# Pinning the low halves of a plain product's weights on VectorE while tiles are converted beside it

## The chip, the cores and the metric

The kernel runs on one core of one Trainium2 chip. The core has a matrix engine (TensorE, PE in the profile), three engines for elementwise work (VectorE or DVE, ScalarE or ACT, GpSimd or POOL) and a queue engine that issues most transfers (SyncE or SP). The metric is the device time of one execution in microseconds.

## The reference

A two-layer encoder over 512 tokens of width 1024, all in float32. Each layer is a mixing block (two kinds of attention in layer 0, a neighbourhood attention in layer 1) followed by the MLP in which the change lies:

```python
def sq_relu_mlp(h, w_up, w_down):
    u = jax.nn.relu(h @ w_up)
    return (u * u) @ w_down

h = h + sq_relu_mlp(rmsnorm(h, norm_ffn[layer]), ffn_w_up[layer], ffn_w_down[layer])
```

`w_up` is 1024 x 4096 and `w_down` 4096 x 1024, so U = (relu(h w_up))² has 32 tiles of 128 columns. The activations are held transposed: a tile is 128 features by 512 tokens.

## The kernel before

**Split operands.** Every float32 operand of a matmul is kept as a high part (rounded to the matmul's format, a copy on ScalarE) and a low part (what the rounding left, a subtraction). A product is three matmuls: high weights by high x, high weights by low x, low weights by high x (`mm3`, L501 to L503). The low part of a weight chunk thus has to be ready one third of the way into the first step that uses it.

**Two kinds of product.** A *plain* product (`product`) takes its weights in chunks of two k tiles by 512 columns: `chunk` loads 128 x 1024 values into `raw` (L190, SyncE, four buffers), copies the high half to `whi` on ScalarE (L212) and subtracts the low half into `wlo` on VectorE (L202); `whi` and `wlo` have three buffers each, shared by all products. A chunk is eight column-and-k steps of three matmuls. A *seven* product (`Seven`) uses a Strassen-like scheme with seven half-size products on pairs of tiles instead of eight (matmuls L388 to L390); its weight chunks are prepared by `seven_chunk` (GpSimd sums L302 to L304, ScalarE L308, VectorE L309), and its result is put together from four banks by `Seven.run` (ScalarE L396, then four VectorE additions L397 to L400).

**The MLP.** `mlp(l)` makes U in three groups and multiplies each group by its rows of `w_down` as it comes. In the third group (z == 2) things overlap. Its `stage` makes the U tiles by seven products. In layer 0 these are 8 tiles for a plain product and then 10 as raw pairs, R; in layer 1, 6 for the plain product, then 8 as raw pairs, R, and at the end 4 more tiles. A raw pair (`raw_evac`) gets a relu and a square on ScalarE (L1148, L1149); a pair that becomes U tiles (`pair_evac`) also gets a high copy on ScalarE (L833) and a low subtraction on VectorE (L830) for each tile. So the last pair before the plain product is a raw one in layer 0 and one with splits in layer 1.

Then the plain product runs in two generators of four column tiles each (8 chunks in all in layer 0, 6 in layer 1; chunks, and their lows, are numbered from 0 here), and beside it `convert` turns the pairs R into operands of the seven product that follows: for each pair three sums on VectorE (L336, L338, L340) and four splits (high on ScalarE L362, low on VectorE L363). One step of `convert` is written after each of the product's column-and-k steps, seven steps to a pair. `ev` adds the product's finished banks to hT (L1265).

**When a low is written.** Planning a product only lists its chunks. When a step asks for chunk i, `weights` starts the loads up to chunk i + 5 and makes chunks up to i + 2 ready: it writes the high copy and the low subtraction of each. At the first step of the plain product that is chunks 0, 1 and 2; after that one chunk at the first step of each chunk.

**The order on an engine.** The written order is not the order that runs. The framework that builds the kernel orders each engine's instructions by its own model of when their operands will be ready, earlier-written ones first, so an instruction that is ready soon can run before ones written earlier. `tc.keep_in_program_order(op)` takes part of that freedom away: it ties `op` behind the instruction written last before it on the same engine (the order only, with no wait for a result). The sums and the low halves of the splits of `convert` are tied in this way (`held`). The lows of the plain product's chunks (L202) are not. An engine runs its instructions in the order that results.

Of the kernel before, what the change touches and what calls it, by code (L numbers as in the profile page):

```python
# [12 lines left out]
ALU = mybir.AluOpType  # L13
# [17 lines left out]
def f32(ap):  # L31
    return ap.bitcast(F32)
# [3 lines left out]
def encoder_kernel(ctx: ExitStack, tc: tile.TileContext, ins, out, dbg=None):  # L36
    nc = tc.nc
    PE, ACT, DVE, POOL, SP = nc.tensor, nc.scalar, nc.vector, nc.gpsimd, nc.sync
# [22 lines left out]
    def nm(s):  # L61
        cnt[0] += 1
        return f"{s}_{cnt[0]}"
# [119 lines left out]
    def chunk(parts, nk, ncol, heads=None, eng=None, first=False):  # L183

        raw = wp.tile([P, 1024], F32, tag="raw", bufs=4, name=nm("raw"))
        r3 = raw[:, 0 : nk * ncol].rearrange("p (k n) -> p k n", k=nk)
        for lo, n, src in parts:
            dst = r3[:, :, lo : lo + n]
            if len(src.shape) == 3:
                SP.dma_start(dst, src)  # L190
            else:
                for k in range(nk):
                    SP.dma_start(dst[:, k].rearrange("p (z m) -> p z m", z=src.shape[2]), src[:, k])
        yield
        hi = wp.tile([P, 1024], F32R, tag="whi", name=nm("whi"))
        lo_ = wp.tile([P, 1024], F32R, tag="wlo", name=nm("wlo"))
        m = nk * ncol
        v = lambda t: t[:, 0:m].rearrange("p (k n) -> p k n", k=nk)
        lows = []

        def low(to, src, high):
            z = lambda: (eng or DVE).tensor_tensor(to, src, f32(high), op=ALU.subtract)  # L202
            if eng:
                z()
            else:
                lows.append(z)

        if heads is None:
            if first:
                DVE.tensor_copy(hi[:, 0:m], raw[:, 0:m])  # L210
            else:
                ACT.activation(hi[:, 0:m], raw[:, 0:m], AF.Copy)  # L212
            low(lo_[:, 0:m], raw[:, 0:m], hi[:, 0:m])
        else:

            na, nb = heads
            hn = ncol // (na + nb)
            r4 = r3.rearrange("p k (h e) -> p k h e", h=hn)
            for e0, n, o in ((0, na, 0), (na, nb, hn * na)):
                z = [v(t)[:, :, o : o + hn * n].rearrange("p k (h e) -> p k h e", h=hn) for t in (hi, lo_)]  # L220
                src = r4[:, :, :, e0 : e0 + n]
                ACT.activation(z[0], src, AF.Copy)
                low(z[1], src, z[0])
        yield v(hi), v(lo_), lows
# [3 lines left out]


    asked, loaded, ready, low_parts = [], [], [], []  # L230
    AHEAD, LOAD = 2, 5

    def plan(*spec, make=None):
# [230 lines left out]
    def tiles(c0, n):  # L464
        return [(c0 + o, min(P, n - o)) for o in range(0, n, P)]
# [749 lines left out]
    def bias_rows():  # L1215
        R, Fi, Fe = Slot(F32), Slot(F32), Slot(F32)
        rpb = ins["od_rpb"][0]
        for qr in range(8):
            SP.dma_start(R.t[16 * qr : 16 * qr + 16, 0:248],
                           rpb.rearrange("h a b -> h (a b)")[:, (7 - qr) * 31 : (7 - qr) * 31 + 248])  # L1220
            yield
        POOL.memset(Fi.t[:, 0:376], NEG)
        POOL.memset(Fe.t[:, 256:512], NEG)
        rv = R.t[:, 0:248].rearrange("p (k d) -> p d k", d=31)
        POOL.tensor_copy(Fi.t[:, 0:376].rearrange("p (j k) -> p j k", k=8)[:, 15:31, :], rv[:, 7:23, :])
        POOL.tensor_copy(Fe.t[:, 0:248].rearrange("p (j k) -> p j k", k=8), rv)
        for _ in range(6):
            yield
        bxv = bx.rearrange("h t (c r) k -> t c r h k", r=8)
        for c in range(16):  # L1230
            SP.dma_start(bxv[0, c].rearrange("r h k -> r h k"), Fi.t[:, (15 - c) * 8 : (15 - c) * 8 + 256])
            yield

            v, off = (1, (7 - c) * 8) if c < 8 else (0, (23 - c) * 8)
            SP.dma_start(bxv[1, c][:, :, 128 * v : 128 * v + 128], Fe.t[:, off : off + 128])
            yield
            SP.dma_start(bxv[1, c][:, :, 128 - 128 * v : 256 - 128 * v], Fe.t[:, 256:384])
            yield
        for s_ in (R, Fi, Fe):
            s_.free()  # L1240
        yield

    def convert(u7, R):
        held = tc.keep_in_program_order
        for kp, raw in enumerate(R):
            yield from u7.sums(kp, raw, DVE, held)
            yield
            yield from u7.split(kp, held)

    def mlp(l, last=None):  # L1250

        stage, ahead, later = first_product(l)
        w = ins["ffn_w_down"][l]
        bias = bias_rows() if l == 0 else iter(())
        beside = lambda m, i: None
        k0 = 0
        for z, n in enumerate(SIZES[l][:3]):  # L1260
            U, R, V = stage(n, *(SIZES[l][3:] if z == 2 else ()))
            up = [s_.pair() for s_ in U]

            def ev(m, b):
                DVE.tensor_tensor(hT[:, m, :], hT[:, m, :], b, op=ALU.add)  # L1265

            gens = [product(w, k0, up, tiles(512 * c, 512), lambda j, b, c=c: ev(4 * c + j, b)) for c in range(2)]
            k0 += n
            work = iter(())
            if z == 2:  # L1270
                u7 = Seven(2 * len(R))
                ids = [u7.plan(w, 256 * m, k0) for m in range(4)]
                if last:
                    beside = last(k0 + 2 * len(R), V)
                reserve[0] = 8
                work = convert(u7, R)
            else:
                ahead()
            for c, gen in enumerate(gens):
                for i, _ in enumerate(gen):  # L1280
                    if z == 0:
                        later(c, i)
                    elif z == 1:
                        next(bias, None)
                    next(work, None)
            for _ in work:
                pass
            reserve[0] = 1
            for s_ in U:
                s_.free()  # L1290
        for m in range(4):

            def evac(w_):
                h2 = hT[:, 2 * m : 2 * m + 2, :]
                DVE.tensor_tensor(h2, h2, w_.t.rearrange("p (z n) -> p z n", z=2), op=ALU.add)

            for i, _ in enumerate(u7.run(ids[m], evac)):
                beside(m, i)
        u7.free()

    mlp(0)


# [273 lines left out]
    def last_mlp():  # L1577
# [77 lines left out]
        def last(k0, tiles_):  # L1655
# [12 lines left out]
            return beside  # L1668

        mlp(1, last)  # L1670
        for run in runs:
            run()
# [56 lines left out]
```

## Time and profile before

| | |
|---|---|
| median of 3 runs | 1183.68 us (1183.31 to 1185.42) |
| span of the profiled execution | 1184.0 us |
| TensorE busy | 1160.5 us |
| VectorE busy | 883.2 us |
| ScalarE busy | 640.3 us |
| GpSimd busy | 526.1 us |

The page gives no time for the profiled execution beside its span, which lies 0.3 us above the median of the runs. In the layer 0 MLP the plain product of the third group begins 510.46 us into the span, in the layer 1 MLP at 1071.96 us.

How to read the lines that follow. A line of a timeline has the start and the length of an instruction in microseconds, the engine, the line of the kernel, the operation, the tile written and those read by the program's names, the shape, and how many were merged into the line; in brackets stands the idle time just before it and what ended it. A line of the table by windows has the window, its length, then for PE, PEld (weight loads), DVE, ACT and POOL the busy time and the number of instructions, the share of TensorE's clock that was granted, the busy share of the DMA engines and their GB/s. A line of waits has the waiting engine and line, who ended the wait, and total, count and longest. Matmuls are pipelined: the length of one is longer than the distance to the next.

### The profile page before, as it was taken

What the parts mean: (1) busy time and instruction counts of PE and PEld (TensorE: products, weight loads), DVE (VectorE), ACT (ScalarE), POOL (GpSimd) and SP (SyncE); (2) the same over time, 40 slices, a digit from 0 to 9 for tenths busy, and PEclk for the clock granted to TensorE, in tenths of its full rate; (3) what the DMA queues carried; (4) which work ended last, traced back from release to release, by engine and by line L of the source; (5) the groups of instructions that cost most, each with busy time, mean ns of one, the idle gap of its engine ahead of it and who ended that gap; (6) DMA issues with size and microseconds to landing.
All of it is one profiled execution on the core that took longest, in us unless ns stands there. A gap on an engine that the chain in (4) does not pass through costs nothing.

```text
span 1184.0 us, 19784 instructions
## 1 busy us (share of the span) xinstructions
PE 1160.5 (98%) x7128; PEld 1021.2 (86%) x7128; DVE 883.2 (75%) x1514; ACT 640.3 (54%) x1081; POOL 526.1 (44%) x662
## 2 busy tenths in 40 slices
PE   9989999999999999999999999999999999999997
PEld 8667778888899899988998998988889989998895
DVE  5788998878967368786884676667996736778975
ACT  4468676664546247562553565555554624666344
POOL 3267343224562377819602232231376625774710
PEclk9999999999999999999999999999999999999998
DMA  7223225212524723225226464433352341322412
GB/s 244 71 54 92 68 78 134 62 56 77 167 86 134 263 70 90 72 90 165 67 72 178 131 184 126 116 112 109 107 165 76 115 134 55 98 64 89 143 36 71
DMA packets 110145, 128.01 MB, mean 108 GB/s; under 512 B 9075, under 2 KB 86816, under 8 KB 110048
## 3 DMA queue, kind: packets, MB, share of 16 engines
q1 hardware_dynamic: 106992, 119.30, 33.5%
q0 software_dynamic: 2304, 6.31, 2.2%
q8 instruction: 56, 0.92, 0.3%
q10 hardware_dynamic: 752, 1.15, 0.3%
q14 instruction: 41, 0.34, 0.1%
HBM read 104.32 MB, written 6.29 MB: 93 GB/s over the span
## 4 chain that ended last, share of the span: by engine, by line
PE 81%; DVE 4%; ACT 1%; issue 1%; POOL 0%; DVEq 0%; ACTq 0%
PE mm L503 8%; PE mm L501 8%; PE mm L502 8%; PE mm L390 4%; PE mm L389 4%; PE mm L388 4%; PE t L388 3%; PE t L389 3%; PE t L390 3%; PE s L502 2%; PE s L503 2%; PE s L501 2%; PE s L390 2%; PE s L388 2%; PE s L389 2%; PE s L997 2%
## 5 line engine op out<-in xcount | busy, mean ns | idle before, releaser
L309 DVE TENSOR_TENSOR wlo<-a,whi 128x896 fp32r<-128x896 f32 x132 | 161.8, 1230 | 83.7 <-ACT whi L308 82.9
L308 ACT ACTIVATE whi<-a 128x896 fp32r<-128x896 f32 x132 | 125.0, 950 | 155.0 <-PE o L502 45.8
L501 PE MATMUL mm<-a,whi 128*128 128x512 f32 x485 | 195.9, 406 | 0.9 <-DVE a L915 0.7
L503 PE MATMUL mm<-a,wlo 128*128 128x512 f32 x485 | 192.1, 397 | 2.5 <-DVE wlo L202 2.5
L502 PE MATMUL mm<-a,whi 128*128 128x512 f32 x485 | 192.5, 397 | 0.1
L202 DVE TENSOR_TENSOR wlo<-raw,whi 128x1024 fp32r<-128x1024 f32 (+4 forms) x117 | 139.3, 1193 | 66.4 <-ACT whi L212 63.9
L212 ACT ACTIVATE whi<-raw 128x1024 fp32r<-128x1024 f32 (+3 forms) x120 | 116.4, 971 | 92.2 <-PE s L502 39.8
L302 POOL TENSOR_TENSOR a<-a 128x128 f32<-128x128 f32 x132 | 85.1, 645 | 173.3 <-DMA a<-in_ffn_w_up_dram 103.9
L303 POOL TENSOR_TENSOR a<-a 128x256 f32<-128x256 f32 x132 | 120.2, 910 | 10.3
L304 POOL TENSOR_TENSOR a<-a 128x128 f32<-128x128 f32 x132 | 115.1, 872 | 10.3
L503 PEld LDWEIGHTS mm<-a,wlo 128*128 128x128 f32 x485 | 91.7, 189 | 23.7 <-DVE wlo L202 3.4
L501 PEld LDWEIGHTS mm<-a,whi 128*128 128x128 f32 x485 | 91.8, 189 | 20.4 <-PE t L972 0.9
L502 PEld LDWEIGHTS mm<-a,whi 128*128 128x128 f32 x485 | 91.9, 190 | 17.4 <-DVE a L545 0.4
L388 PE MATMUL mm<-a,whi 128*128 128x256 f32 x370 | 103.9, 281 | 0.0
L389 PE MATMUL mm<-a,whi 128*128 128x256 f32 x370 | 103.9, 281 | 0.0
L390 PE MATMUL mm<-a,wlo 128*128 128x256 f32 x370 | 103.7, 280 | 0.0
L1005 POOL TENSOR_SCALAR p<-p,ti 128x512 f32<-128x512 f32 x64 | 46.2, 724 | 92.3 <-DVE ti L1004 81.1
L1430 POOL TENSOR_SCALAR p<-p,ti 128x256 f32<-128x256 f32 x64 | 35.6, 567 | 104.8 <-DVE ti L1429 91.8
L388 PE MATMUL t<-a,whi 128*128 128x256 f32 x264 | 74.2, 281 | 0.0
L389 PE MATMUL t<-a,whi 128*128 128x256 f32 x264 | 74.1, 281 | 0.0
L390 PE MATMUL t<-a,wlo 128*128 128x256 f32 x264 | 73.9, 280 | 0.0
L390 PEld LDWEIGHTS mm<-a,wlo 128*128 128x128 f32 x370 | 69.6, 188 | 0.2 <-DVE wlo L309 0.2
(338 smaller groups left out, 3210.8 us busy)
## 6 DMA issues: line engine op xcount, KB each, us to landing
a<-in_ffn_w_up_dram SPq DMA_DIRECT2D x104, 256.0 KB
raw<-in_ffn_w_down_dram SPq DMA_DIRECT2D x46, 512.0 KB
raw<-in_od_w_qkv_dram SPq DMA_DIRECT2D x64, 128.0 KB
a<-in_ffn_w_down_dram SPq DMA_DIRECT2D x28, 256.0 KB
raw<-in_ffn_w_up_dram SPq DMA_DIRECT2D x12, 512.0 KB
raw<-in_ev_w_in_dram SPq DMA_DIRECT2D x12, 384.0 KB
a<-a SPq DMA_DIRECT2D x18, 256.0 KB
bias<-bx SPq DMA_DIRECT2D x16, 256.0 KB
```

What stands on the lines that cost most here:

```text
L202: z = lambda: (eng or DVE).tensor_tensor(to, src, f32(high), op=ALU.subtract)
L212: ACT.activation(hi[:, 0:m], raw[:, 0:m], AF.Copy)
L303: POOL.tensor_tensor(r[:, 4:6], r[:, 2:3].to_broadcast([P, 2, P]), r[:, 0:7:6], op=ALU.add)
L304: POOL.tensor_tensor(r[:, 7], r[:, 3], r[:, 5], op=ALU.subtract)
L308: ACT.activation(hi[:, 0:896], raw[:, 128:1024], AF.Copy)
L309: DVE.tensor_tensor(lo[:, 0:896], raw[:, 128:1024], f32(hi[:, 0:896]), op=ALU.subtract)
L388: PE.matmul(o, wh, x[:, 0], start=kp == 0 and n in (0, 1, 3, 5), stop=False, skip_group_check=True)
L389: PE.matmul(o, wh, x[:, 1], start=False, stop=False, skip_group_check=True)
L390: PE.matmul(o, wl, x[:, 0], start=False, stop=kp == self.np - 1, skip_group_check=True)
L501: PE.matmul(o, wh, xh, start=first, stop=False)
L502: PE.matmul(o, wh, xl, start=False, stop=False)
L503: PE.matmul(o, wl, xh, start=False, stop=last)
```

## The change

While `convert` runs beside the plain product of the third group, the subtraction that makes a plain chunk's low half is tied to its written place on VectorE as well. A flag, `pinned`, is raised after `convert` is set up and before the product's loop, and lowered when the loop and what is left of `convert` are done. The seven product's chunks are not affected, nor are chunks whose lows run on GpSimd, which the third group does not have.

```diff
@@ -199,7 +199,11 @@
         lows = []
 
         def low(to, src, high):
-            z = lambda: (eng or DVE).tensor_tensor(to, src, f32(high), op=ALU.subtract)
+            def z():
+                op = (eng or DVE).tensor_tensor(to, src, f32(high), op=ALU.subtract)
+                if pinned[0]:
+                    tc.keep_in_program_order(op)
+
             if eng:
                 z()
             else:
@@ -228,6 +232,7 @@
 
 
     asked, loaded, ready, low_parts = [], [], [], []
+    pinned = [False]
     AHEAD, LOAD = 2, 5
 
     def plan(*spec, make=None):
@@ -1274,6 +1279,7 @@
                     beside = last(k0 + 2 * len(R), V)
                 reserve[0] = 8
                 work = convert(u7, R)
+                pinned[0] = True
             else:
                 ahead()
             for c, gen in enumerate(gens):
@@ -1286,6 +1292,7 @@
             for _ in work:
                 pass
             reserve[0] = 1
+            pinned[0] = False
             for s_ in U:
                 s_.free()
```

## The prediction

> **What bounds the kernel now.** I read the page's engine table first, then TensorE's waits by line, then the instructions in order of time around the two stages that the change touches.
>
> ```profile
> span 1184.0 us, 19784 instructions
> PE 1160.5 (98%) x7128; PEld 1021.2 (86%) x7128; DVE 883.2 (75%) x1514; ACT 640.3 (54%) x1081; POOL 526.1 (44%) x662
> ```
>
> TensorE is busy for 98% of the span: whatever keeps it fed costs nothing, and nearly every microsecond in which it waits is a microsecond of the result. In the layer 1 stage of the change it waits once (waits of TensorE from 1060 to 1115 us; then its timeline, start and length in us):
>
> ```profile
> PE mm L503 <- DVE wlo L202: 2.2, 1, 2.2
> ```
>
> ```profile
> 1099.95 0.40 PE L502 MATMUL mm<-a,whi 128*128 128x512 f32 x1
> 1102.58 0.79 PE L503 MATMUL mm<-a,wlo 128*128 128x512 f32 x1 [2.23 <-DVE wlo L202]
> 1103.17 0.63 PE L501 MATMUL mm<-a,whi 128*128 128x512 f32 x1
> ...
> 1106.09 0.40 PE L502 MATMUL mm<-a,whi 128*128 128x512 f32 x1
> ```
>
> ```profile
> 1099.18:1102.59 3.41, 1.18 (x6) 0.60 (x5) 3.41 (x6) 1.65 (x3) 2.95 (x4) 1.00 0.51 163
> 1102.59:1106.00 3.41, 3.41 (x8) 2.73 (x9) 3.41 (x5) 0.10 (x1) 3.17 (x5) 0.50 0.56 171
> ```
>
> The third matmul of plain chunk 5 waits for its weights' low half. Undisturbed matmuls start 0.231 us apart (eight from 836.04 to 837.89 us, quoted below), so the wait costs 2.63 - 0.23 = 2.40 us. In the next 3.41 us the granted clock (the column after POOL) is 0.50: the eight starts from 1102.58 to 1106.09 us take 3.51 instead of 1.85, another 1.66 us. **The old stall is worth 4.06 us**, and there is nothing else in these stages to gain. The layer 0 stage shows no wait at all.
>
> **The change, part by part.** No arithmetic, DMA or buffer is added. What is added is eight order edges in layer 0 and six in layer 1, one for each L202 low of the plain chunks: each low must follow on VectorE whatever was written before it. The sums and splits already had such edges, and so could never run before a low written ahead of them; only the lows could run early. So I ask which lows run early now.
>
> *Layer 0.* Lows 0, 1 and 2 are written at the product's first step, after the last pair's evacuation (L397 to L400).
>
> ```profile
> 507.65 1.23 DVE L202 TENSOR_TENSOR wlo<-raw,whi 128x1024 fp32r<-128x1024 f32 x1 [2.27 <-ACT whi L212]
> ...
> 510.88 0.68 DVE L397 TENSOR_TENSOR a<-a,mm 128x512 f32<-128x512 f32 x1
> 511.66 0.69 DVE L398 TENSOR_TENSOR a<-a,mm 128x512 f32<-128x512 f32 x1
> ...
> 513.40 0.41 DVE L399 TENSOR_TENSOR a<-a,mm 128x256 f32<-128x256 f32 x1
> 513.73 0.69 DVE L336 TENSOR_TENSOR a<-a 128x512 f32<-128x512 f32 x1
> 514.34 0.68 DVE L400 TENSOR_TENSOR a<-a,s 128x512 f32<-128x512 f32 x1
> ```
>
> ```profile
> 510.46 0.40 PE L501 MATMUL s<-a,whi 128*128 128x512 f32 x1
> ```
>
> ```profile
> 509.61 0.36 ACT L396 ACTIVATE a<-mm 128x256 f32<-128x256 f32 x1
> ```
>
> Low 0 runs at 507.65 us, before the whole evacuation, and is ready when the plain product starts at 510.46. Pinned, it comes after L400. The adds then run back to back: L396 ends at 509.97, the four adds are 0.68 + 0.69 + 0.41 + 0.68 = 2.46 us, some 0.15 more for hand-overs, so L400 ends near 512.6; low 0 takes 1.23 and is ready at 513.85. TensorE in written order would reach that low after two matmuls, at 510.93. But the framework's order lets later matmuls pass where it foresees the wait. This trace has the same situation in layer 1's first product:
>
> ```profile
> 836.04 0.40 PE L501 MATMUL mm<-a,whi 128*128 128x512 f32 x1
> ...
> 837.66 0.39 PE L502 MATMUL s<-a,whi 128*128 128x512 f32 x1
> 837.89 0.95 PE L522 MATMUL t<-ones,acc 128*128 128x1 f32 x8
> 838.70 0.95 PE L503 MATMUL mm<-a,wlo 128*128 128x512 f32 x3
> ```
>
> All eight high-half matmuls of the four column tiles go first, 1.85 us of cover. No more can pass, since each bank's next matmul is written after its low one. I take that: TensorE runs out at 512.31, and the stall is 513.9 - 512.3 = **1.6 us**. Bounds: 3.0 us without the cover; 1.3 if the hand-overs vanish and L397 starts with the bank instead of L396. Whether the clock drops is bounded by the nearest rows: the 2.23 us idle above halved it, this one did not (its timeline row, then its window):
>
> ```profile
> 68.95 1.20 PE L997 MATMUL s<-a,a 128*128 128x512 f32 x4 [1.36 <-DVE a L624]
> ```
>
> ```profile
> 68.00:72.00 4.00, 3.05 (x13) 2.36 (x13) 3.88 (x5) 1.63 (x4) 2.92 (x2) 1.00 0.69 213
> ```
>
> 1.6 is nearer to 1.36: I take 0, bound 1.66. Lows 1 and 2 follow at 1.2 us each and chunks are 24 x 0.231 = 5.55 us apart, so they are in time.
>
> *Layer 1.* Here the last pair becomes two U tiles, so its relu, square and two splits (L1148, L1149, L833, L830) are written before low 0 too.
>
> ```profile
> 1068.81 1.23 DVE L202 TENSOR_TENSOR wlo<-raw,whi 128x1024 fp32r<-128x1024 f32 x1 [2.06 <-ACT whi L212]
> 1069.95 2.11 DVE L830 TENSOR_TENSOR a<-a,a 128x512 fp32r<-128x512 f32 x2
> 1071.98 0.67 DVE L397 TENSOR_TENSOR a<-a,mm 128x512 f32<-128x512 f32 x1
> ```
>
> ```profile
> 1075.88 0.68 DVE L336 TENSOR_TENSOR a<-a 128x512 f32<-128x512 f32 x1
> 1076.48 0.68 DVE L400 TENSOR_TENSOR a<-a,s 128x512 f32<-128x512 f32 x1
> ...
> 1080.76 1.23 DVE L202 TENSOR_TENSOR wlo<-raw,whi 128x1024 fp32r<-128x1024 f32 x1 [2.81 <-ACT whi L212]
> 1081.91 1.28 DVE L830 TENSOR_TENSOR a<-a,a 128x512 fp32r<-128x512 f32 x2
> 1083.89 3.04 DVE L363 TENSOR_TENSOR a<-a,a 128x512 fp32r<-128x512 f32 x4 [0.70 <-ACT a L362]
> ```
>
> ```profile
> 1077.25 1.06 ACT L1148 ACTIVATE a<-a 128x1024 f32<-128x1024 f32 x1
> ...
> 1078.74 1.04 ACT L1149 ACTIVATE a<-a 128x1024 f32<-128x1024 f32 x1
> ...
> 1080.63 1.14 ACT L833 ACTIVATE a<-a 128x512 fp32r<-128x512 f32 x2
> ```
>
> ```profile
> 1071.96 0.39 PE L501 MATMUL s<-a,whi 128*128 128x512 f32 x1
> ```
>
> Freed of low 0, the earlier L830 pair ends near 1071.2; L397 to L400 (2.5 us) end near 1073.7; relu 1.06, square 1.04, split highs 1.14, with 0.2 of hand-overs, end at 1077.1; the second L830 (0.7) at 1077.85; low 0 at 1079.05. The product starts at 1071.96, its cover ends at 1073.81: a stall of **5.3 us**. Bounds: 4.3 (adds straight behind the bank, no hand-overs) and 7.8 (no cover: 6.7; one more 1.1 us ScalarE piece in the chain). The clock: idle well over 2.23 us, so **1.66 us** again, bounds 0 and 3.3 (two such stretches).
>
> The old stall goes. Its low 5 is last of a VectorE chain:
>
> ```profile
> 1101.05 1.47 DVE L202 TENSOR_TENSOR wlo<-raw,whi 128x1024 fp32r<-128x1024 f32 x1
> ```
>
> Lows 1 and 2 now end at 1081.4, the three sums from there take at most 2.1 (0.68 us for the L336 row above, the two of half its size no more), the splits start at 1083.5, where they start now (1083.89), since the idle 2.81 us and the queue behind low 3 vanish. From there to low 5 the trace has 17.16 us, plus low 3, which moves into the stretch (1.23): low 5 ends at 1103.4. TensorE, 7 us later, asks for it at 1100.2 + 6.96 = 1107.1: 3.7 us of cover. **-4.06 us.**
>
> Weight loads: a raw buffer is freed by its low, so the loads of chunks 4 and 5 are issued later on SyncE's queue, and seven-product loads queue behind them.
>
> ```profile
> 1070.06 4.26 SPq L190 DMA_DIRECT2D raw<-in_ffn_w_down_dram  x2
> ```
>
> ```profile
> 1083.76 1.05 ACT L212 ACTIVATE whi<-raw 128x1024 fp32r<-128x1024 f32 x1
> ```
>
> Chunk 4's load, issued at 1070.06, was used by 1083.76, so it needs at most 13.7 us; issued at 1079.1 it is there by 1092.8, and its matmuls start at 1071.96 + 4 x 5.55 + 6.96 = 1101.1. Nothing, with 8 us of cover.
>
> The other later lows move by a place or two of VectorE's work (the rows show 0.4 to 1.3 us a place) against chunks of 5.55 us: nothing.
>
> **Sum:** 1.6 + 5.3 + 1.66 - 4.06 = +4.5 us. The profiled span of 1184.0 becomes 1188.5; the three runs' median, 1183.68, lies 0.3 below the span, so I forecast **1188.2 us**. Its own bounds, without the rivals below, are about 1186 to 1191.
>
> **Rivals.** *No cover.* The framework keeps TensorE in written order. For it: most of this stage's matmuls are in that order, and at 1102.58 nothing passed. Against: the 836 us rows, where the wait was foreseeable as here. Then 3.0 + 6.7 of stalls, two half-clock stretches (3.0 us idle is above 2.23), less 4.06: +9.0, 1192.7. [...]
>
> *The old stall stays as well.* VectorE is slowed in this stage (the L336 of 0.68 us above takes longer later on) and uses up the 3.7 us.
>
> ```profile
> 1097.85 0.94 DVE L336 TENSOR_TENSOR a<-a 128x512 f32<-128x512 f32 x1
> ```
>
>  Then nothing is won back: +8.6, 1192.3.
>
> *The first three lows are not bound,* since they would be traced before the flag rises, and only lows 3 to 5 move. Then no new stall arises, and low 3 no longer stands before the L830 pair: that pair starts with its L833 data near 1081.3 instead of 1081.91, low 5 comes 0.6 us sooner, and if the remaining 1.6 us idle leaves the clock alone, 1.66 more is won: 1181.4 to 1183.1. It decides at the moment of tracing: if low 0 stands ahead of L397, this is the case. Against: planning a product only lists its chunks, and the first step of the loop, behind the flag, makes chunks 0 to 2 ready.
>
> **Chances.** Forecast 0.69, no cover 0.13, old stall stays 0.10, first lows unbound 0.08. What this kernel's measurement can tell from no change is about 0.2%, 2.4 us, up to 1186.05. The unbound case is mostly inside it (0.06 of 0.08; 0.02 faster), and 0.06 of the forecast's share lies in it, with both stalls near their lower bounds; another 0.02 faster for bounds that I misjudge. Faster 0.04, same 0.12, slower 0.84. The range for 8 in 10 leaves out the unbound case and what lies above the case without cover: 1185.6 to 1193.0.
>
> **What would show it.** In layer 0: low 0 after L400, near 512.6 us; eight high matmuls; an idle of 1.6 us before the first low matmul, clock still 1.00. In layer 1: low 0 after the second L830 pair; idle of about 5.3 us, then a stretch at 0.50; no wait for chunk 5's low. Wrong, if TensorE idles elsewhere, if low 0 still precedes L397, or if matmuls from other chunks fill the gap.

## The result and the profile after

The changed kernel takes 1190.65 us (median of 5 runs, 1188.6 to 1191.61) against 1183.68: a ratio of 1.0057, 95% interval 1.0046 to 1.0068. Measured a second time beside other runs (e9 below) it was 1189.21 us, ratio 1.0039 (1.0026 to 1.0053). It is slower by 3 to 8 us; the forecast was 4.5. Its profiled execution has a span of 1188.5 us, where the prediction's sum gave 1188.5. That these agree to the digit is luck: as the table of stages below shows, the two stages grew by 5.2 us together and not by 4.5, and in this run layer 0's stage starts 0.65 us earlier (509.81 against 510.46).

New lines of code stand before the rest, so lines of the changed kernel carry higher numbers: L506 to L508 are the former L501 to L503, L203 is L202, L402 to L405 are L397 to L400, L835 is L830, L838 is L833, L368 is L363, L1153 and L1154 are L1148 and L1149, L393 to L395 are L388 to L390. TensorE's waits of the changed kernel from 490 us to the end (line, releaser, total, count, longest):

```profile
PE s L508 <- DVE wlo L203: 6.7, 2, 5.2
```

Two waits for a low half, and no wait for chunk 5's; the other rows of this view, left out here, are single waits of 0.2 us. Where they stand, in the timelines of TensorE and VectorE, layer 0 first:

```profile
509.81 0.40 PE L506 MATMUL s<-a,whi 128*128 128x512 f32 x1
...
511.20 0.40 PE L506 MATMUL o<-a,whi 128*128 128x512 f32 x1
511.44 0.39 PE L507 MATMUL o<-a,whi 128*128 128x512 f32 x1
513.26 0.51 PE L508 MATMUL s<-a,wlo 128*128 128x512 f32 x1 [1.43 <-DVE wlo L203]
```

```profile
509.35 0.69 DVE L402 TENSOR_TENSOR a<-a,mm 128x512 f32<-128x512 f32 x1 [4.62 <-ACT a L401]
...
511.38 0.69 DVE L405 TENSOR_TENSOR a<-a,s 128x512 f32<-128x512 f32 x1
511.99 3.49 DVE L203 TENSOR_TENSOR wlo<-raw,whi 128x1024 fp32r<-128x1024 f32 x3
```

The evacuation runs whole, then lows 0 to 2 in a row. TensorE runs all eight high-half matmuls, s to o, and then stands still until low 0 is there. Layer 1, in VectorE's, ScalarE's and TensorE's timelines:

```profile
1074.19 0.69 DVE L405 TENSOR_TENSOR a<-a,s 128x512 f32<-128x512 f32 x1
1077.81 1.29 DVE L835 TENSOR_TENSOR a<-a,a 128x512 fp32r<-128x512 f32 x2 [2.93 <-ACT a L838]
1079.02 3.49 DVE L203 TENSOR_TENSOR wlo<-raw,whi 128x1024 fp32r<-128x1024 f32 x3
...
1083.95 2.22 DVE L368 TENSOR_TENSOR a<-a,a 128x512 fp32r<-128x512 f32 x4
```

```profile
1074.97 1.06 ACT L1153 ACTIVATE a<-a 128x1024 f32<-128x1024 f32 x1 [0.24 <-DVE a L405]
1076.06 1.06 ACT L1154 ACTIVATE a<-a 128x1024 f32<-128x1024 f32 x1
1077.15 1.15 ACT L838 ACTIVATE a<-a 128x512 fp32r<-128x512 f32 x2
```

```profile
1073.05 0.39 PE L506 MATMUL s<-a,whi 128*128 128x512 f32 x1
...
1074.67 0.39 PE L507 MATMUL o<-a,whi 128*128 128x512 f32 x1
1080.29 0.79 PE L508 MATMUL s<-a,wlo 128*128 128x512 f32 x1 [5.24 <-DVE wlo L203]
```

Before low 0 stands the chain the prediction named: last addition, relu, square, two split highs on ScalarE, two split lows on VectorE. VectorE is idle for 2.93 us of it with lows 0 to 2 tied behind, whose high halves ScalarE (L216, the former L212) had written by 1074.42 us.

The clock, in the table by windows (window, length, then busy time and count for PE, PEld, DVE, ACT and POOL, then the granted clock). The first two windows lie in layer 0, the others in layer 1:

```profile
511.27:514.69 3.42, 1.99 (x9) 1.33 (x8) 3.32 (x5) 2.26 (x3) 0.00 (x0) 1.00 0.09 14
514.69:518.10 3.41, 3.41 (x16) 2.72 (x16) 3.34 (x7) 1.66 (x3) 0.00 (x0) 1.00 0.93 278
1074.47:1077.89 3.42, 0.58 (x3) 0.16 (x1) 0.49 (x2) 3.11 (x5) 0.44 (x1) 1.00 0.00 0
1077.89:1081.30 3.41, 1.01 (x2) 0.83 (x3) 3.41 (x5) 1.04 (x2) 0.00 (x0) 0.50 0.00 0
1081.30:1084.71 3.41, 3.41 (x9) 2.64 (x8) 3.34 (x7) 1.26 (x2) 0.00 (x0) 0.50 0.81 273
1084.71:1088.10 3.39, 3.39 (x16) 2.76 (x15) 2.99 (x5) 2.02 (x3) 0.80 (x1) 1.00 0.35 117
```

Layer 0's 1.43 us left it alone. After layer 1's wait began, two windows were at half clock, 1077.89 to 1084.71 us: 2.40 us of them lie inside the wait, which ends at 1080.29, and 4.42 us follow it. In them matmuls start 0.43 us apart (1082.16 to 1084.30 us), where 0.23 us lies between two at full clock.

**A ruler for single runs.** Execution times of one kernel differ by up to 5 us from run to run (28 of before, beside e7: 1182.7 to 1187.57 us), so a term of 1 or 2 us is hard to see in them. But each stage has a sharp start and end on TensorE: the first matmul of the plain product, and the first of the seven product after it. For the changed kernel they are the first row of each TensorE fence above and these two, the ends of the two stages:

```profile
555.91 0.28 PE L393 MATMUL s<-a,whi 128*128 128x256 f32 x1
...
1113.94 0.28 PE L393 MATMUL s<-a,whi 128*128 128x256 f32 x1
```

So its stages last 555.91 - 509.81 = 46.10 and 1113.94 - 1073.05 = 40.89 us. The layer 1 stage of e7, the version without any wait there, will serve as the base; these are its start and its end:

```profile
1072.04 0.39 PE L501 MATMUL s<-a,whi 128*128 128x512 f32 x1
...
1105.38 0.28 PE L388 MATMUL s<-a,whi 128*128 128x256 f32 x1
```

It lasts 33.34 us. Worked out in the same way from each run's profile:

| run | layer 0 stage, us | layer 1 stage, us | from layer 0's stage to layer 1's, us |
|---|---|---|---|
| before | 44.41 | 37.40 | 517.1 |
| e0, before again | 44.41 | 36.25 | 517.1 |
| the change | 46.10 | 40.89 | 517.1 |
| e9, the change again | 46.19 | 40.58 | 517.1 |
| e1, lows 0 to 2 free | 44.40 | 34.61 | 517.2 |
| e2, only lows 0 to 2 pinned | 46.16 | 40.68 | 517.1 |
| e3, layer 0 alone | 46.10 | 37.82 | 517.1 |
| e4, layer 1 alone | 44.41 | 41.68 | 517.1 |
| e5, tied to the last addition | 44.40 | 34.64 | 517.1 |
| e6, extra matmuls in the gap | 46.10 | 38.86 | 517.1 |
| e7, slower conversion | 44.40 | 33.34 | 517.2 |
| e8, e1 with e7 | 44.40 | 33.34 | 517.1 |

Everything between the two stages is the same to 0.2 us in all twelve profiles, and what follows layer 1's stage to 0.1 us in all but e7 and e8. So the change acts in these two stages and nowhere else. What comes before layer 0's stage varies: it starts between 508.5 and 511.3 us, and the last section shows a reason for part of that.

### The profile page after: what moved, and what is told of

It reads as the page before. It is cut to its first block, busy times and chain, and to the rows that moved or that the text cites. A ratio compares the mean times of both kernels' runs of the same rounds, so it can differ in the third digit from the quotient of the medians.

```text
span 1188.5 us, 19785 instructions
## 1 busy us (share of the span) xinstructions
PE 1160.6 (98%) x7128; PEld 1021.2 (86%) x7128; DVE 882.1 (74%) x1514; ACT 641.0 (54%) x1081; POOL 522.5 (44%) x662
## 3 DMA queue, kind: packets, MB, share of 16 engines
q10 hardware_dynamic: 752, 1.15, 0.3%
## 4 chain that ended last, share of the span: by engine, by line
PE 82%; DVE 3%; ACT 2%; issue 1%; POOL 0%; DVEq 0%; ACTq 0%
PE mm L506 8%; PE mm L508 8%; PE mm L507 8%; PE mm L395 3%; PE mm L394 3%; PE mm L393 3%; PE t L393 3%; PE s L508 3%; PE t L394 3%; PE t L395 3%; PE s L507 3%; PE s L506 2%; PE s L395 2%; PE s L393 2%; PE s L394 2%; PE t L508 2%
## 5 line engine op out<-in xcount | busy, mean ns | idle before, releaser
L506 PE MATMUL mm<-a,whi 128*128 128x512 f32 x485 | 195.3, 404 | 0.9 <-DVE a L920 0.7
L508 PE MATMUL mm<-a,wlo 128*128 128x512 f32 x485 | 191.0, 395 | 0.3 <-DVE wlo L203 0.3
L203 DVE TENSOR_TENSOR wlo<-raw,whi 128x1024 fp32r<-128x1024 f32 (+4 forms) x117 | 138.2, 1187 | 59.0 <-ACT whi L216 58.7
L216 ACT ACTIVATE whi<-raw 128x1024 fp32r<-128x1024 f32 (+3 forms) x120 | 116.4, 971 | 98.2 <-PE s L507 36.3
L307 POOL TENSOR_TENSOR a<-a 128x128 f32<-128x128 f32 x132 | 83.4, 632 | 169.9 <-DMA a<-in_ffn_w_up_dram 115.9
L308 POOL TENSOR_TENSOR a<-a 128x256 f32<-128x256 f32 x132 | 122.7, 930 | 10.3
L309 POOL TENSOR_TENSOR a<-a 128x128 f32<-128x128 f32 x132 | 112.4, 852 | 10.4
L508 PEld LDWEIGHTS mm<-a,wlo 128*128 128x128 f32 x485 | 91.3, 189 | 20.9 <-DVE wlo L203 0.7
L506 PEld LDWEIGHTS mm<-a,whi 128*128 128x128 f32 x485 | 91.3, 188 | 20.2 <-PE t L977 0.8
L393 PE MATMUL mm<-a,whi 128*128 128x256 f32 x370 | 103.9, 281 | 0.0
L395 PE MATMUL mm<-a,wlo 128*128 128x256 f32 x370 | 103.8, 280 | 0.0
L393 PE MATMUL t<-a,whi 128*128 128x256 f32 x264 | 74.2, 281 | 0.0
L395 PE MATMUL t<-a,wlo 128*128 128x256 f32 x264 | 73.9, 280 | 0.0
L395 PEld LDWEIGHTS mm<-a,wlo 128*128 128x128 f32 x370 | 69.6, 188 | 0.2 <-DVE wlo L314 0.2
```

Of the source, the lines that this page charges most:

```text
L203: op = (eng or DVE).tensor_tensor(to, src, f32(high), op=ALU.subtract)
L308: POOL.tensor_tensor(r[:, 4:6], r[:, 2:3].to_broadcast([P, 2, P]), r[:, 0:7:6], op=ALU.add)
L309: POOL.tensor_tensor(r[:, 7], r[:, 3], r[:, 5], op=ALU.subtract)
L393: PE.matmul(o, wh, x[:, 0], start=kp == 0 and n in (0, 1, 3, 5), stop=False, skip_group_check=True)
L395: PE.matmul(o, wl, x[:, 0], start=False, stop=kp == self.np - 1, skip_group_check=True)
L506: PE.matmul(o, wh, xh, start=first, stop=False)
```

## The experiments

**e0: the kernel before, once more.**

> The kernel before, unchanged, to see span and time side by side. The changed kernel's runs lie 2.1 us above their spans (1190.65 against 1188.5); the only profile of before has a span of 1184.0, but its timed runs have a median of 1183.68. Theory: the offset is the same 2.1 us, so a usual run of before has a span near 1181.6, and the profiled one was an unlucky one in which the wait for chunk 5's low was long and halved the clock (4.06 us); in usual runs that stall costs 1 to 2 us. Rival: the offset is 0 for this kernel and every run has the stall at 4.06 us; spans near 1183.7.

The median was 1184.93 us, the profile's time 1185.18 and its span 1183.1: the offset of 2.1 us is the same for both kernels. The spans of the runs of before beside it lay between 1180.6 and 1184.8, so the first profile, with 1184.0, was one of the longer runs, and the rival of an offset of 0 falls. The wait for chunk 5's low was there, but not the half clock (timeline, then windows):

```profile
1103.30 0.50 PE L503 MATMUL mm<-a,wlo 128*128 128x512 f32 x1 [2.66 <-DVE wlo L202]
```

```profile
1098.96:1102.37 3.41, 1.68 (x8) 1.02 (x6) 3.41 (x6) 1.33 (x3) 3.05 (x6) 1.00 0.48 160
1102.37:1105.79 3.42, 2.49 (x11) 2.06 (x12) 3.42 (x5) 0.77 (x1) 3.26 (x4) 1.00 0.40 129
```

So the theory holds for the offset and, in this one profile, for the clock. It was wrong on the wait, which was not shorter (2.66 against 2.23 us). Measured against e7's stage without any wait (33.34 us), the old stall is worth 37.40 - 33.34 = 4.06 us in the first profile and 36.25 - 33.34 = 2.91 in this one, where 1 to 2 us were expected.

**e1: the first three lows free, the later ones pinned.**

```diff
-                pinned[0] = True
...
                     next(work, None)
+                    pinned[0] = z == 2
```

> The flag is raised only after the product's first step, so lows 0 to 2 are free and only the later ones are pinned. Theory (the whole loss is in lows 0 to 2): no new wait at the start of either plain product; low 3 of layer 1 goes behind the L835 pair, which comes up to 0.6 us sooner: between 1181.4 and 1183.7 us. Rival (any pinned low delays the product, since VectorE's pieces queue behind it): about as slow as the change, 1188 to 1191.

1183.6 us, ratio 0.9988 (0.9978 to 0.9997). Layer 0's stage is back at 44.40, and layer 1's is 34.61: no new wait, and the old one shrinks (TensorE's waits in e1, from 480 us on):

```profile
PE mm L508 <- DVE wlo L203: 1.0, 1, 1.0
```

The rival falls. Pinning the later lows is even a small gain, as the prediction's third rival had it: the old stall shrinks to 34.61 - 33.34 = 1.3 us.

**e2: only the first three pinned.**

```diff
                     next(work, None)
+                    pinned[0] = False
```

> The flag is lowered after the product's first step: only lows 0, 1 and 2 of each stage are pinned, the later ones are free. Theory (pinning the later lows neither costs nor gains anything once the first three are pinned): the same as the change, within 0.7 us, with the same two waits of 1.4 and 5.2 us. Rival (keeping the later lows in place is what removes the old wait for chunk 5's low, so without it that wait comes back): 1 to 3 us slower than the change, with a third wait near 1107 us.

1189.46 us, ratio 1.0043 (1.0031 to 1.0056), beside e9's 1.0039; stages 46.16 and 40.68. Layer 1 has one wait of 5.2 us and none near 1107 us (TensorE's waits in e2 from 1060 to 1120 us):

```profile
PE s L508 <- DVE wlo L203: 5.2, 1, 5.2
```

The rival falls. All of the loss comes from lows 0 to 2, and the old wait vanishes without the later pins: TensorE, 7 us later, no longer meets it.

**e3 and e4: one layer at a time.**

```diff
-                pinned[0] = True
+                pinned[0] = l == 0
```

(e4 with `l == 1`.)

> The flag is raised in layer 0 alone. Theory (a wait of 1.43 us and a loss of 1.6 us in layer 0, with the clock left at 1.00): 1.6 us over before, 1185.3; layer 1 as before, its wait for chunk 5's low included. Rival (the layer 0 wait is taken up later, by slack in VectorE's work): 1183.7.

> The flag is raised in layer 1 alone. Theory (the two layers add up): the change without the 1.6 us of layer 0, 1189.0, with a wait of 5.2 us, one or two half-clock stretches after it, and no wait for chunk 5's low. Rival (the layers interact, so that layer 0's shift decides when the clock drops): off this sum by more than 1 us.

e3: 1187.38 us, ratio 1.0025 (1.0016 to 1.0034), about 3 us where 1.6 was expected. Its layer 0 stage grew by 1.69, as in the change, so the rival falls, and its layer 1 stage stands at 37.82, near the first profile's 37.40 and not e0's 36.25. In the profiled run the rest of the time is there: the old wait, 2.66 us long as in e0, this time halved the clock (windows of e3):

```profile
1100.66:1104.07 3.41, 0.85 (x4) 0.72 (x5) 3.41 (x5) 1.47 (x2) 3.25 (x5) 1.00 0.11 37
1104.07:1107.49 3.42, 3.42 (x10) 2.65 (x9) 3.42 (x4) 0.00 (x0) 3.19 (x5) 0.50 0.69 230
```

e4: 1190.7 us, ratio 1.0044 (1.003 to 1.0058); layer 0 44.41, layer 1 41.68, one wait of 5.2 us and none for chunk 5's low. By the stages the layers add up, but for the clock: 46.10 in e3 and 41.68 in e4, against 46.10 and 40.89 in the change. By the times the sum of both alone, 1.0069, is above the change's 1.0057 and 1.0039. One reason is that the old stall, which the change removes, cost more in e3 than in e0 (37.82 against 36.25 us of stage), because it halved the clock there.

e4 also missed its figure, 1190.7 where 1189.0 was expected, and its layer 1 stage was 0.8 us longer than the change's. The clock accounts for that. The wait is the same (e4's TensorE timeline):

```profile
1077.56 0.79 PE L508 MATMUL s<-a,wlo 128*128 128x512 f32 x1 [5.24 <-DVE wlo L203]
```

But the half clock, shown in the last section, lasts until 1083.70, 6.14 us past the wait, where the change had 4.42. In all four profiles with this wait, the base of 33.34, the wait's 5.39 and half of the half-clock time behind it give the stage to 0.12 us: 41.80 against 41.68 measured in e4, 40.94 against 40.89 in the change, 40.71 against 40.68 in e2 (3.96 us behind it), 40.64 against 40.58 in e9 (3.81 us). Whether layer 0's shift has a part in when the clock drops, as e4's rival says, these runs can't tell: where there is half clock near 75 us, it begins at another place in each profile, at 75.18 us in before and 74.96 in e0, which are the same kernel, at 74.37 in the change and 73.56 in e5.

**e5: lows 0 to 2 of layer 1 behind the last addition.**

```diff
-                if pinned[0]:
+                if tied[0]:
+                    tied[0] -= 1
+                    tc.add_manual_dep(op.ins, add4[0].ins.name, mybir.DependencyInfo(
+                        mybir.DependencyClass.NoSync, mybir.DependencyReason.DATA), reason="tie")
+                elif pinned[0]:
                     tc.keep_in_program_order(op)
...
-            DVE.tensor_tensor(r[:, 1:3], r[:, 1:3], two(bk[3]), op=ALU.add)
+            add4[0] = DVE.tensor_tensor(r[:, 1:3], r[:, 1:3], two(bk[3]), op=ALU.add)
...
-                pinned[0] = True
+                pinned[0] = l == 1
+                tied[0] = 3 if l else 0
```

> As e4 (layer 1 alone), but lows 0 to 2 are tied behind the last addition of the evacuation instead of behind the last pair's two L835 splits. Theory (the 5.2 us wait is the chain relu, square, split highs, L835 that stands before low 0, and not the pinning as such): low 0 is ready about 1.3 us after the last addition, the wait falls to 1.0 to 1.8 us as in layer 0, the clock stays at 1.00, and the wait for chunk 5's low, up to 2.7 us in before, shrinks because TensorE is later: within 1.5 us of before, 1183 to 1186. Rival (VectorE's queue as a whole is late, whatever stands before low 0): a wait over 4 us and 1189 to 1191, as e4.

1183.73 us, ratio 0.999 (0.9981 to 0.9999). VectorE's order of the three lows and the two splits is exchanged (VectorE and TensorE in e5; lines here stand nine higher than in before, so L839 is L830 and L512 is L503; L203 is L202):

```profile
1073.05 0.69 DVE L409 TENSOR_TENSOR a<-a,s 128x512 f32<-128x512 f32 x1
1073.65 3.49 DVE L203 TENSOR_TENSOR wlo<-raw,whi 128x1024 fp32r<-128x1024 f32 x3
1077.06 1.29 DVE L839 TENSOR_TENSOR a<-a,a 128x512 fp32r<-128x512 f32 x2
```

```profile
1074.93 0.50 PE L512 MATMUL s<-a,wlo 128*128 128x512 f32 x1 [1.01 <-DVE wlo L203]
```

The 5.2 us become 1.0, the clock stays at 1.00 after it, and the old wait is gone: the later pins, kept here, had shrunk it to 1.0 us in e1, and TensorE is now over 1 us later. The chain in front of low 0 was the cause, not the pin as such.

**e6: TensorE kept busy in the gap.**

```diff
                     next(work, None)
+                    if l == 1 and z == 2 and c == 0 and i == 0:
+                        idle_work(18, mmb())
```

The added matmuls multiply ones into a free bank that nothing reads; the trace has two records for each.

> The changed kernel with 18 extra matmuls of ones, of no use to the result, in the layer 1 gap, so that TensorE is busy while it waits. Theory (part of the loss is the half clock, 6.8 us of it after the wait in the profile of the change): granted clock 1.00 after the gap, 1.7 to 2.2 us less than the change: near 1188.3. Rival (the clock is no part of the loss, or the extra matmuls delay the product as much): 1190 to 1191.

Windows and the matmul after the gap, in e6:

```profile
1075.30:1078.70 3.40, 3.40 (x33) 3.40 (x32) 0.88 (x2) 3.09 (x5) 0.91 (x2) 1.00 0.00 0
1078.70:1082.10 3.40, 2.19 (x12) 1.54 (x11) 2.88 (x4) 1.64 (x3) 0.00 (x0) 1.00 0.00 0
1082.10:1085.50 3.40, 3.40 (x17) 2.77 (x16) 3.33 (x6) 0.68 (x2) 0.00 (x0) 1.00 0.70 220
```

```profile
1081.70 0.50 PE L508 MATMUL s<-a,wlo 128*128 128x512 f32 x1 [1.22 <-DVE wlo L203]
```

With useless work in the gap the clock stays at 1.00. The first low matmul starts 1081.70 - 1074.46 = 7.24 us after the stage does, exactly as in the change (1080.29 - 1073.05), so the extra matmuls neither delay nor hasten it. Yet layer 1's stage is 38.86 us instead of 40.89 and 40.58: the half clock costs 1.7 to 2.0 us. (Of the 6.8 us at half clock that the expectation puts after the wait, only 4.42 follow it.) The times (1189.16 us, ratio 1.0032, 1.002 to 1.0044) point the same way. Their interval lies just below the change's first one but overlaps that of e9, so it is the stage that decides.

**e7: a version that beats both.** The pins are left off, and layer 1's conversion is written at three steps in four.

```diff
-                    next(work, None)
+                    if l == 0 or z < 2 or i % 4 != 3:
+                        next(work, None)
```

> The kernel before (no pins on the lows), with the conversion of layer 1 written slower: every fourth step of the product writes no step of it, so low 5 is written after 18 pieces of the conversion instead of 24. Theory (the old wait comes from low 5 standing behind too much conversion on VectorE): no wait for chunk 5's low, 2.9 us less, and the half clock that some runs pay too: 1180.5 to 1181.6. Rival (VectorE has too much work before that point in any order, or the conversion is then late for the seven product): 1184 to 1185.5, with the wait moved to L390.

1182.54 us, ratio 0.9973 (0.9964 to 0.9981): 3.2 us less by the ratio; layer 1's stage is 2.9 us shorter than e0's, of which 0.5 us is given back behind it, as the rival feared. Low 5 moves forward on VectorE (timeline of e7), 6 us earlier than in before, and layer 1 has no wait for it:

```profile
1094.92 1.21 DVE L202 TENSOR_TENSOR wlo<-raw,whi 128x1024 fp32r<-128x1024 f32 x1
```

The gain is the expected one against the runs of before beside it (1185.42); the absolute time is a microsecond above the figure, as before itself was.

**e8: e1 and e7 together.**

> e7's slower writing together with e1's pins on the lows after the first three. Theory (both attack the same wait, and e7 alone removes it): as e7, 1180.5 to 1181.6. Rival (the pins add a gain of their own by keeping low 3 behind the L835 pair): another 0.5 to 1 us below e7.

1183.34 us, ratio 0.9983 (0.9974 to 0.9992): 0.8 us above e7 where the same was expected, and no gain, so the rival falls: layer 1's stage is the same 33.34 us, but the seven product behind it now waits 1.0 us for its own lows (waits of TensorE from 1060 us to the end, e8, then e7):

```profile
PE s L395 <- DVE wlo L314: 1.0, 2, 0.6
```

```profile
PE s L390 <- DVE wlo L309: 0.2, 1, 0.2
```

**e9: the changed kernel again.**

> The changed kernel once more, beside e2 and with more runs. Theory: 1.0057 of before as measured first, 6 to 7 us. For the clock: after the 5.2 us wait at least one stretch of 3.41 us at half clock in the profile, two where the wait covers over 2 us of two stretches of the grid of 3.41 us in which the clock is set. Rival for the clock (its drop depends on the length of the wait alone): always two.

1189.21 us, ratio 1.0039, below the 6 to 7 us expected; stages 46.19 and 40.58. Its 5.2 us wait, too, brought two stretches at half clock. It covered 2.21 us of one stretch and 3.02 of the next, so theory and rival both say two here. All four profiles that have the wait show two, e4 among them, where it reached only 0.69 us into the second: that fits the rival and not the theory, though of e3 and e0, with the same shorter wait of 2.66 us, only e3 shows half clock after it.

## Why the prediction was right, step by step

| term of the sum | predicted, us | measured, us |
|---|---|---|
| layer 0: wait for low 0 | 1.6 | 1.69 (stage 46.10 - 44.41) |
| layer 1: wait for low 0 | 5.3 | 5.39 (starts 5.62 apart, less 0.23) |
| half clock after it | 1.66 | 2.16 (40.89 - 33.34 - 5.39) |
| old stall removed | -4.06 | -4.06 in the first profile, -2.91 in e0 |
| sum | 4.5 | 5.2 against the first profile, 6.3 against e0 |

The times gave 6.7 us by the first ratio and 4.6 by the second, on both sides of the last row.

*Which lows move:* right; e1 and e2 show that the loss is in lows 0 to 2 alone.

*Layer 0's chain and its cover:* right. The evacuation took 509.35 to 512.07 us, 0.23 of it between its four additions (the prediction put 0.15 for these hand-overs, an estimate), eight matmuls passed, and the clock stayed. That the clock would stay was a choice by the nearer of two rows; a row of e4 in the last section agrees, in which the clock stayed at 1.00 after 1.87 us idle.

*Layer 1's chain:* right to 0.1 us in total. Its pieces ran in the order given, and e5, which takes the relu, square and splits from in front of low 0, cuts the wait from 5.2 to 1.0 us.

*The clock after it:* that the wait halves the clock was right, and the size was low: there are two stretches, the first of them mostly inside the wait, and 4.42 us at half clock behind it cost some 2.2 us. The prediction took 1.66 with a bound of 3.3. What it judged by, the length of one wait, did not decide here: e3 and e0 had the same wait of 2.66 us with and without the drop.

*The old stall goes:* right, and for the reason given. Chunk 5's low ended at 1102.41 + 1.48 = 1103.89 us in the changed kernel (1103.4 predicted; the stage started 1.1 us later in this run), and TensorE came to it at 1108.82 without a wait (VectorE, then TensorE):

```profile
1102.41 1.48 DVE L203 TENSOR_TENSOR wlo<-raw,whi 128x1024 fp32r<-128x1024 f32 x1
```

```profile
1108.82 0.39 PE L508 MATMUL mm<-a,wlo 128*128 128x512 f32 x1
```

Its size was taken from the one profiled execution, in which it had halved the clock; in e0 it did not, and it is worth 1.15 us less there. That and the second half-clock stretch raise the sum from 4.5 to 6.3 us, near the first measurement. The second, 4.6, lies at the forecast; part of that agreement is luck, since by the stages two terms of the sum were off by 0.5 and 1.15 us.

*The base:* the prediction set the median beside the span as if they were the same quantity. A time lies 2.1 us above the span of the same run, so the profiled run, with its span of 1184.0, would have had a time near 1186.1: it was a longer run than the median of 1183.68. Leaving out the offset and taking a longer run for a usual one nearly cancel, which is luck.

*Weight loads, later lows:* nothing, as said; neither a new wait nor a longer stretch shows.

*The rivals:* no cover is excluded by the eight matmuls, the old stall staying by the waits. The third, that low 0 is not bound, is excluded for the change; as an experiment (e1) it gave a time 1.4 us below before by its ratio, inside the 0.6 to 2.3 us worked out for it.

## What to carry to other kernels

An order edge to "whatever was written last" can cost what that last instruction waits for: here the same pin cost 1.7 us behind an addition and 7.5 us, with the clock, behind a chain through another engine, and nothing on the later lows (e1, e2). Before pinning a small, early-ready operation, look in the timeline of before at what it overtakes. And where a late operand is the complaint, thinning out the work written in front of it (e7) won 3.2 us, where the best pins tried (e1, e5) won 1.2 to 1.4.

## What the hardware showed that was not expected

In the profiles of before and of the change, the changes of TensorE's granted clock lie whole multiples of 3.41 us apart. In the change half clock begins at 74.37, 1077.89 and 1183.70 us: 1003.52 us from the first to the second is 294 times 3.4133, and 105.81 to the third is 31 times; the first lasts 3.41 us, the second 6.83, and the third reaches the end of the span. In before it begins at 75.18, 1102.59 and 1177.68 us: 1027.41 us is 301 times 3.4133, and 75.09 is 22 times; the first two last 3.41 us. In these profiles and in e0, e3, e4 and e5 a drop went with how much of the stretch of 3.41 us before it TensorE was idle, not with the length of one wait. The same wait of 2.66 us was followed by half clock in e3, where 2.56 us of it fell into one such stretch (0.85 busy), and not in e0, where it lay in two, with 1.73 us and 0.93. The wait near 72 us (2.39 us long in before) gives the nearest pair of rows, one without a drop and one with it (e4, then e5):

```profile
69.94:73.35 3.41, 1.54 (x7) 0.93 (x5) 2.99 (x10) 2.42 (x3) 0.59 (x1) 1.00 0.19 58
73.35:76.76 3.41, 2.92 (x13) 2.30 (x14) 3.24 (x11) 2.47 (x7) 0.13 (x1) 1.00 0.00 0
```

```profile
70.14:73.56 3.42, 1.41 (x7) 0.82 (x5) 3.00 (x10) 2.29 (x3) 0.49 (x1) 1.00 0.18 58
73.56:76.97 3.41, 3.04 (x7) 2.46 (x8) 2.89 (x8) 2.33 (x6) 0.00 (x0) 0.50 0.00 0
```

After 1.87 us idle of 3.41 the clock stayed at 1.00, after 2.01 the next stretch was at 0.50. Cut into such stretches from end to end, the profiles of before and of the change agree: the six at full clock with the most idle time (2.23, 2.39 and 2.60 us in before, 2.35, 2.84 and 3.41 in the change) were each followed by half clock, and every other one, idle for 1.43 us at most, by full clock. The drop of 3.41 us in before's layer 1 cost 1.66 us (eight matmul starts in 3.51 us instead of 1.85). A drop falls on some runs and not on others: the three profiles without it near 72 us (e2, e3, e4) are the three whose layer 0 stage starts earliest, at 508.5 to 509.0 us, and the others start at 509.8 to 511.3. For a stretch that is itself at half clock these figures do not hold, and what decides there stays open: in e4 one with only 0.69 us idle was followed by another at 0.50, and so was one with 2.40 us idle in the change (1077.89 to 1081.30), while the next one there, 0.00 us idle, was followed by full clock. The rows of e4, from within its wait on:

```profile
1073.46:1076.87 3.41, 0.00 (x0) 0.00 (x0) 1.79 (x3) 2.54 (x4) 0.00 (x0) 1.00 0.00 0
1076.87:1080.28 3.41, 2.72 (x6) 2.15 (x7) 3.41 (x4) 0.16 (x1) 0.00 (x0) 0.50 0.43 143
1080.28:1083.70 3.42, 3.42 (x10) 2.64 (x8) 3.35 (x8) 1.26 (x2) 0.00 (x0) 0.50 0.71 240
```
